# One stage's hand-written TensorE order in a hybrid HGRN2 and pooling layer: mean squares placed apart from the pool projections, first two head-branch products interleaved, kept weights later, banks taken in reverse

## The chip, the cores and the metric

The kernel runs on one core of one Trainium2 chip. The metric is device time in microseconds (us) of one launch, lower is better; a time stands beside others as the median of several runs. Five engines work side by side, each through its own queue of instructions in order, and they meet only through semaphores: TensorE (PE in the profile: matmuls from on-chip memory into PSUM banks), VectorE (DVE), ScalarE (ACT), GpSimd (POOL) and SyncE (SP, which here only issues transfers).

## The reference

One layer of a decoder in float32, 1024 tokens of width 1024 with 16 learned tokens ahead of them:

```python
u = rmsnorm(h, mix_norm_pre[l])
proj = u @ w_in[l]
q, f_logit, i_in, g_out, v_pool, gate_a, gate_b = jnp.split(proj, cuts, axis=-1)
a = hgrn2(q, f_logit, i_in, g_out, lbs[l], hgrn_out_norm[l])     # 4 heads of 128
p = multiscale_pool(v_pool, pool_proj[l], pool_scale[l])         # 4 groups of 128
z = (jax.nn.sigmoid(gate_a) * (a @ w_branch_hgrn[l])
     + jax.nn.sigmoid(gate_b) * (p @ w_branch_pool[l]))
h = h + rmsnorm(z @ w_out[l], mix_norm_post[l])
u = rmsnorm(h, ffn_norm_pre[l])
gt = causal_dwconv(u @ ffn_w_gate[l], ffn_conv_w[l], ffn_conv_b[l])
y = (jax.nn.gelu(gt, approximate=True) * (u @ ffn_w_up[l])) @ ffn_w_down[l]
h = h + rmsnorm(y, ffn_norm_post[l])
```

Inside `hgrn2` a head's output is divided by its root mean square over the 128 channels, `o * lax.rsqrt(jnp.mean(o * o, axis=-1, keepdims=True) + EPS)`, then multiplied by a gain and a sigmoid. `multiscale_pool` takes windowed means of `v_pool` and multiplies each group by a 128x128 matrix. Only the order of this work and the PSUM banks it lands in are touched here.

## The kernel before, in words

Every large product is made of three single-pass matmuls: both operands are split into a rounded high part and a rest (`whi`, `wlo` for weights; `hi`, `lo` for activations), and high x high, high x low and low x high are added in PSUM. The split of a weight block is a cast on ACT and a subtraction on DVE. Channels lie on the 128 partitions, and the 1026 tokens that matter lie along the free dimension in three chunks of 342 columns, so one product of this stage fills three PSUM banks.

The stage in question lies between about 385 and 570 us. It is emitted by one loop that reads the string `ORDER`, token by token. On PE the program order is kept as written; the order on ACT, DVE, SP and POOL is chosen by a scheduler at build time from the same program. The tokens:

- `h0` to `h3` take the next of twelve steps of a head: load, start block (L722), six levels of the recurrence (L693, L699), transpose (L754), state (L771), output (L784, L791, L792), and **mean squares**: six matmuls with a matrix of constants into three banks (L801, L802), then on ACT a logarithm per bank (L803) and one exponential (L804), each behind a table load, then a multiplication on DVE (L805).
- `G` with p, q, r, s: a quarter each of a gate projection (18 matmuls, L207, L208, L211); its sigmoids are L625 on ACT.
- `PP0` to `PP3`: pool projections, nine matmuls each; three copies on ACT (L842) and three subtractions on DVE (L843) read the three banks and free them.
- `BB0` to `BB7` and `BA0` to `BA7`: the products with `w_branch_pool` and `w_branch_hgrn`, 36 matmuls each, here in halves a and b (BB) or whole (BA). DVE multiplies each of the three banks by a gate (L881), and for BA adds the other branch (L1186). `sa0` to `sa3` split a head's finished output for BA (ACT and DVE, L835, L836).
- `w0` to `w5`: weights of the next layer part are prepared early and stored away ("kept"): casts on ACT (L924), sums and subtractions on DVE (L922, L925), stores on SP (L939).

The weights of BB and BA come two products to a block: a load on SP (L162), a cast on ACT (L163), a subtraction on DVE (L164). The buffers `wraw`, `whi` and `wlo` have three places each, shared with the kept weights. PSUM has eight banks in this stage; a new bank is the next in turn. Behind BA stands the mix product with `w_out` (results `pm`, from L187 to L189): its weights are loaded by SP (L1219), cast by ACT (L1226), and subtracted by POOL (L1228); ACT and DVE split `z` for it (L1130, L1131). Rows of `x` and of the learned tokens for the residual are loaded by SP beside them (L1269, L1267).

Of the kernel before, what the change touches and what calls it, by code (L numbers as in the profile page):

```python
# [12 lines left out]
ALU = mybir.AluOpType  # L13
# [40 lines left out]
AHEAD = 3  # L54

ORDER = ("h0 h1 PVp0 PVq0 h0 PVr0 h1 PVs0 h0 PVp1 h1 PVq1 h0 PVr1 h1 PVs1 h0 sp0 PVp2 h1 PVq2 h0 sp1 PVr2 h1 PVs2 "
# [4 lines left out]
POOLED = ()  # L61
VLOAD = 8
TRUNC = False
# [6 lines left out]
def trunk_kernel(ctx: ExitStack, tc: tile.TileContext, x, meta_tokens, mix_norm_pre,  # L70
# [4 lines left out]
    act, dve, pool_e, pe = nc.scalar, nc.vector, nc.gpsimd, nc.tensor  # L75
# [20 lines left out]
    def nm(s):  # L96
        cnt[0] += 1
        return f"{s}_{cnt[0]}"
# [7 lines left out]
    def bank(name="ps"):  # L106
        return stage["ps", "p"].tile([P, 512], F32, tag="ps", name=nm(name))
# [39 lines left out]
    def wsplit(src, n_k, n_c, eng=dve):  # L147
        raw = wst.tile([P, n_k * n_c], F32, tag="wraw", name=nm("wraw"), bufs=NRAW, padded_shape=[P, 1024])
        with tc.issue_after(stage["after"].ins) if "after" in stage else nullcontext():
            stage["load"] = nc.sync.dma_start(raw.rearrange("p (k c) -> p k c", k=n_k), src)  # L150
        hi = wst.tile([P, n_k * n_c], F32R, tag="whi", name=nm("whi"), padded_shape=[P, 1024])
        lo = wst.tile([P, n_k * n_c], F32R, tag="wlo", name=nm("wlo"), padded_shape=[P, 1024])
        act.copy(hi, raw)
        eng.tensor_tensor(lo, raw, rr(hi), ALU.subtract)
        return [(hi.rearrange("p (k c) -> p k c", k=n_k), lo.rearrange("p (k c) -> p k c", k=n_k))]
# [11 lines left out]
    class Loader:  # L167
# [10 lines left out]
        def next(self):  # L178
            self.at += 1
            return self.got[self.at - 1]  # L180

    def wblock(w, k0, n_k, c0, n_c):
        return w[k0 * P : (k0 + n_k) * P, c0 : c0 + n_c].rearrange("(k p) c -> p k c", p=P)

    def mm3(ps, a, b, first, last):
        (ahi, alo), (bhi, blo) = a, b
        pe.matmul(ps, ahi, bhi, start=first, stop=False)  # L187
        pe.matmul(ps, ahi, blo, start=False, stop=False)  # L188
        pe.matmul(ps, alo, bhi, start=False, stop=last)  # L189

    def proj(*a, **k):
        for banks in proj_parts(*a, **k):
            pass
        return banks

    def proj_parts(w, col, n_k, xs, chunks, ws=None, name="pj", by_bank=0, cuts=()):

        if ws is None:
            ws, = wsplit(wblock(w, 0, n_k, col, P), n_k, P)
        whi, wlo = ws  # L200
        banks = [bank(name) for _ in chunks]
        for k in range(n_k - by_bank):
            if k in cuts:
                yield banks
            for (lo, n), ps in zip(chunks, banks):
                xhi, xlo = xs(k, lo, n)
                pe.matmul(ps[:, :n], whi[:, k, :], xhi, start=(k == 0), stop=False)  # L207
                pe.matmul(ps[:, :n], whi[:, k, :], xlo, start=False, stop=False)  # L208
            for (lo, n), ps in zip(chunks, banks):
                xhi, _ = xs(k, lo, n)  # L210
                pe.matmul(ps[:, :n], wlo[:, k, :], xhi, start=False, stop=(k == n_k - 1))  # L211
        for (lo, n), ps in zip(chunks, banks):
            for k in range(n_k - by_bank, n_k):
                mm3(ps[:, :n], (whi[:, k, :], wlo[:, k, :]), xs(k, lo, n), False, k == n_k - 1)
        yield banks
# [609 lines left out]
    def pool_split(g):  # L825
        w = POOL_WINDOWS[g]
        cur, vp = pooled[g]
        if w > T0 + 1:
            dve.tensor_scalar(cur[:, T0 : T0 + 1], cur[:, T0 : T0 + 1], float(w) / (T0 + 1), None, ALU.mult)
        dve.scalar_tensor_tensor(cur[:, T0:L], cur[:, T0:L], 1.0 / w, vp[:, T0:L], ALU.mult, ALU.subtract)  # L830
        pin[g] = split(cur[:, T0:L], "pl")

    def split(src, name, eng=dve):
        hi, lo_ = slot(TQ, F32R, name + "h"), slot(TQ, F32R, name + "l")
        act.copy(hi, src)  # L835
        eng.tensor_tensor(lo_, src, rr(hi), ALU.subtract)  # L836
        return hi, lo_
# [10 lines left out]
    sas, sbs, z = {}, {}, {}  # L848
# [44 lines left out]
    def job(kind, i):  # L893
        if kind == "G":
            return (wblock(WIN, 0, KD, CG + i * P, P), KD, u_q, CH_Q, lambda r: post_g(i, r))
        if kind == "PV":
            return (wblock(WIN, 0, KD, CV + i * P, P), KD, u_all, CH_ALL, lambda r: post_pv(i, r))
        if kind == "PP":
            return (pool_proj[0, i].rearrange("(k c) d -> c k d", k=1), 1,
                    lambda k, lo, n: (pin[i][0][:, lo : lo + n], pin[i][1][:, lo : lo + n]), CH_Q,  # L900
                    lambda r: post_pp(i, r))
        if kind == "BA":
            return (wblock(w_branch_hgrn[0], 0, HEADS, i * P, P), HEADS, a_x, CH_Q, lambda r: post_branch(sas, i, r))
        return (wblock(w_branch_pool[0], 0, HEADS, i * P, P), HEADS, p_x, CH_Q, lambda r: post_branch(sbs, i, r))
# [32 lines left out]
    def pay():  # L937
        while owed:
            nc.sync.dma_start(*owed.pop(0))  # L939

    def keep_first(u):
        raw = wst.tile([P, 1024], F32R, tag="wraw", name=nm("wraw"), bufs=NRAW)
        src = rr(raw).rearrange("p (k c) -> p k c", k=KD)
        nc.sync.dma_start(src, wblock(ffn_w_gate[0], 0, KD, 2 * u * P, P))
        keep(((u, "P1"), src[:, :4]), ((u, "P2"), src[:, 4:]), lo=raw)
# [82 lines left out]
    with tc.manual_schedule(engines={E.Activation, E.DVE, E.PE}):  # L1028
# [59 lines left out]
        for h in range(EARLY_G):  # L1088
            src, n_k, xs, chunks, post = job("G", h)
# [51 lines left out]
    with tc.manual_schedule(engines={E.PE}):  # L1141
        for kind, i in order:
            if kind == "sp":
                pool_split(i)
                continue
            if kind == "w":
                keep_first(i) if i < EARLY else next(keeps[i - EARLY])
                continue
            if kind == "sa":
                ahl[i] = split(heads[i]["o"], "a")  # L1150
                continue
            if kind == "h":
                if i not in gens:
                    gens[i] = head_steps(i)
                next(gens[i], None)
                if not loader.at and "after" in stage:
                    loader.ahead()
                continue
            kind, part = kind.rstrip("abpqrs"), kind[-1]
            src, n_k, xs, chunks, post = job(kind, i)  # L1160
            if part in "qr":
                next(halves_of[kind, i])
                continue
            if part in "bs":
                banks = next(halves_of[kind, i])
                loader.ahead()
                pay()
                after[kind, i] = post(banks)
                continue
            if kind in ("BA", "BB"):  # L1170
                load_gate(sas if kind == "BA" else sbs, kind == "BB", i)
            ws = loader.next()
            if (kind, i) == ("BA", KD - 1):
                z0 = [split_z(0, k) for k in range(ZA)]
            if part in "ap":
                halves_of[kind, i] = proj_parts(None, 0, n_k, xs, chunks, ws=ws, name="p" + kind.lower(),
                                                cuts=(n_k // 2,) if part == "a" else range(n_k // 4, n_k, n_k // 4))
                next(halves_of[kind, i])
                continue
            banks = proj(None, 0, n_k, xs, chunks, ws=ws, name="p" + kind.lower(),  # L1180
                         by_bank=2 if (kind, i) == ("BA", KD - 1) else 0)
            loader.ahead()
            pay()
            after[kind, i] = post(banks)
            if kind == "BA":
                dve.tensor_tensor(sas[i], sas[i], sbs[i], ALU.add)  # L1186
                z[i] = sas[i]
# [384 lines left out]
    with tc.manual_schedule(engines={E.PE, E.Activation, E.DVE, E.Pool}):  # L1572
        for i in (1, "m", 0):
            R[i] = Row(0 if i == "m" else HALO + i * P, HALO if i == "m" else P, pair("pm"))
        for c in range(3):
            for at in range(KD - LAST):
                first_, _, then_ = SEAM[c][at].rpartition("|")
# [130 lines left out]
    with tc.manual_schedule(engines={E.Activation, E.DVE}):  # L1708
        for s_ in range(3):
            banks = [[bank("pd") for _ in range(NT)] for _ in range(2)]  # L1710
# [24 lines left out]
    banks = [bank("pd") for _ in range(NT)]  # L1735
# [74 lines left out]
```

## Time and profile before

| what | value |
|---|---|
| runs | 1316.93, 1314.59, 1315.93 us; median 1315.93 |
| profiled execution | 1315.67 us, span 1314.0 us |
| TensorE busy | 1291.8 us, 98% of the span |
| VectorE, ScalarE, GpSimd busy | 962.9, 524.2, 355.1 us (73%, 40%, 27%) |
| mean granted TensorE clock | 0.997 |

The profiled execution is 0.26 us under the median and 1.67 us longer than its span. In rows of instructions the columns are: start in us, duration, engine, line, operation, result and operands, how many were merged, and in square brackets the idle time of that engine just before and what ended it. In the list of waits they are: engine and line that waited, what released it, us in total, times, longest. In a table by stretches each engine has its busy time and in brackets its instructions, and PEclk is the granted clock.

### The profile page before, as it was taken

What the parts mean: (1) busy time and instruction counts of PE and PEld (TensorE: products, weight loads), DVE (VectorE), ACT (ScalarE), POOL (GpSimd) and SP (SyncE); (2) the same over time, 40 slices, a digit from 0 to 9 for tenths busy, and PEclk for the clock granted to TensorE, in tenths of its full rate; (3) what the DMA queues carried; (4) which work ended last, traced back from release to release, by engine and by line L of the source; (5) the groups of instructions that cost most, each with busy time, mean ns of one, the idle gap of its engine ahead of it and who ended that gap; (6) DMA issues with size and microseconds to landing.
All of it is one profiled execution on the core that took longest, in us unless ns stands there. A gap on an engine that the chain in (4) does not pass through costs nothing.

```text
span 1314.0 us, 21961 instructions
## 1 busy us (share of the span) xinstructions
PE 1291.8 (98%) x8650; PEld 1139.7 (87%) x8650; DVE 962.9 (73%) x1293; ACT 524.2 (40%) x905; POOL 355.1 (27%) x307
## 2 busy tenths in 40 slices
PE   8999999999999999999999999999999999999998
PEld 7799899998998898978898888888888888888887
DVE  6768965454775877775588999888998985455758
ACT  5554433332245546236564222232232323444443
POOL 3015333130000000070045555654755652000000
PEclk9999999999999899999999999999999999999999
DMA  8135642325513557797677777668776799666644
GB/s 275 42 106 164 193 162 98 121 90 163 164 68 135 162 177 249 253 334 260 235 267 236 200 209 184 170 193 193 169 181 154 156 260 298 208 224 225 226 174 160
DMA packets 143801, 247.62 MB, mean 188 GB/s; under 512 B 11000, under 2 KB 75164, under 8 KB 143698
## 3 DMA queue, kind: packets, MB, share of 16 engines
q1 hardware_dynamic: 127026, 213.42, 48.4%
q0 software_dynamic: 12064, 24.38, 10.9%
q10 hardware_dynamic: 4608, 8.41, 1.7%
q8 instruction: 68, 1.11, 0.3%
q14 instruction: 35, 0.29, 0.1%
HBM read 174.11 MB, written 95.09 MB: 205 GB/s over the span
## 4 chain that ended last, share of the span: by engine, by line
PE 58%; DMA 3%; ACT 1%; DVE 1%; POOL 1%; issue 0%; SPq 0%; DVEq 0%; ACTq 0%; POOLq 0%
PE P L308 11%; PE P L307 11%; PE P L310 11%; PE pd L187 5%; PE pd L188 5%; PE pd L189 5%; PE pm L188 2%; PE pm L189 2%; PE pm L187 2%; POOL wlo L1228 1%; DMA kept4l<-wraw 1%; DMA wlos<-wlo 1%; PE pba L207 1%; PE pba L208 1%; PE pt L1280 1%; PE pba L211 1%
## 5 line engine op out<-in xcount | busy, mean ns | idle before, releaser
L308 PE MATMUL P<-v,whi 128*128 128x512 f32 (+2 forms) x408 | 140.7, 353 | 0.0
L307 PE MATMUL P<-v,whi 128*128 128x512 f32 (+2 forms) x408 | 140.7, 352 | 0.0
L310 PE MATMUL P<-v,wlo 128*128 128x512 f32 (+2 forms) x424 | 135.1, 349 | 0.0
L278 POOL TENSOR_TENSOR swa<-wraw,wraw 128x512 f32<-128x512 f32 x32 | 48.2, 1507 | 190.4 <-DMA wraw<-in_ffn_w_gate_dram 71.2
L252 ACT CAST whi<-wraw 128x512 fp32r<-128x512 f32 x90 | 53.1, 618 | 101.7 <-PE P L308 86.9
L1520 DVE TENSOR_TENSOR rot<-wraw,rot 128x1024 fp32r<-128x1024 f32 x31 | 37.9, 1224 | 72.3 <-ACT rot L1519 72.3
L307 PEld LDWEIGHTS P<-v,whi 128*128 128x128 f32 x408 | 76.7, 188 | 10.4
L308 PEld LDWEIGHTS P<-v,whi 128*128 128x128 f32 x408 | 76.6, 188 | 10.2
L310 PEld LDWEIGHTS P<-v,wlo 128*128 128x128 f32 x424 | 74.0, 188 | 10.8
L189 PE MATMUL pd<-rot 128*128 128x512 f32 x274 | 82.5, 388 | 0.0
L188 PE MATMUL pd<-rot 128*128 128x512 f32 x274 | 82.5, 388 | 0.0
L187 PE MATMUL pd<-rot 128*128 128x512 f32 x274 | 81.9, 388 | 0.1
L253 DVE TENSOR_TENSOR wlo<-wraw,whi 128x512 fp32r<-128x512 f32 x86 | 75.2, 896 | 2.7 <-ACT whi L252 2.7
L252 ACT CAST whi<-swa 128x512 fp32r<-128x512 f32 x64 | 38.1, 618 | 90.9 <-PE P L308 80.3
L253 DVE TENSOR_TENSOR wlo<-swb,whi 128x512 fp32r<-128x512 f32 x64 | 67.0, 1054 | 8.8 <-ACT whi L252 8.7
L1519 ACT CAST rot<-wraw 128x1024 fp32r<-128x1024 f32 x31 | 32.7, 1054 | 90.7 <-PE pd L189 89.4
L307 PE MATMUL P<-uhi,whi 128*128 128x258 f32 (+2 forms) x240 | 68.6, 303 | 0.1
L308 PE MATMUL P<-ulo,whi 128*128 128x258 f32 (+2 forms) x240 | 68.4, 303 | 0.0
L252 ACT CAST whi<-swb 128x512 fp32r<-128x512 f32 x64 | 38.1, 618 | 69.1 <-PE P L308 64.6
L307 PE MATMUL P<-t2h,whi 128*128 128x258 f32 (+2 forms) x228 | 65.3, 304 | 0.3 <-DVE sg L864 0.3
L307 PE MATMUL P<-t4h,whi 128*128 128x258 f32 (+2 forms) x228 | 65.5, 304 | 0.0
L308 PE MATMUL P<-t4l,whi 128*128 128x258 f32 (+2 forms) x228 | 65.4, 304 | 0.0
(386 smaller groups left out, 3841.4 us busy)
## 6 DMA issues: line engine op xcount, KB each, us to landing
wraw<-in_w_in_dram SPq DMA_DIRECT2D x36, 512.0 KB, 4.7
yt<-ysum SPq DMA_DIRECT2D x33, 512.0 KB, 5.5
wraw<-in_ffn_w_gate_dram SPq DMA_DIRECT2D x26, 512.0 KB, 6.2
wraw<-in_ffn_w_up_dram SPq DMA_DIRECT2D x22, 512.0 KB, 6.7
wsum<-in_ffn_w_down_dram SPq DMA_DIRECT2D x22, 512.0 KB, 8.3
wraw<-in_w_out_dram SPq DMA_DIRECT2D x18, 512.0 KB, 5.1
ysum<-ys SPq DMA_DIRECT2D x11, 768.0 KB, 5.7
sa<-sscr SPq DMA_DIRECT2D x16, 513.0 KB, 6.4
```

The source lines that it names most:

```text
L187: pe.matmul(ps, ahi, bhi, start=first, stop=False)
L188: pe.matmul(ps, ahi, blo, start=False, stop=False)
L189: pe.matmul(ps, alo, bhi, start=False, stop=last)
L207: pe.matmul(ps[:, :n], whi[:, k, :], xhi, start=(k == 0), stop=False)
L252: act.copy(hi, src)
L253: (pool_e if 4 <= i < 2 * self.early else dve).tensor_tensor(lo, src, rr(hi), ALU.subtract)
L278: pool_e.tensor_tensor(s1, a21, a22, ALU.add)
L307: pe.matmul(d, whi[:, k, :], xh[:, c : c + w], start=(k == 0 and onto is None), stop=False, **go)
L308: pe.matmul(d, whi[:, k, :], xl[:, c : c + w], start=False, stop=False, **go)
L310: pe.matmul(x[:, o : o + w], wlo[:, k, :], xh[:, c : c + w], start=False, stop=(k == 3), **go)
L1519: act.copy(hi, src)
L1520: dve.tensor_tensor(lo, src, rr(hi), ALU.subtract)
```

## The change

Three edits. The string `ORDER` is rewritten from the last quarters of G on. The mean squares of heads 0 and 1 no longer follow a pool projection: quarters of G or a level stand ahead of them, and the projections follow closer on each other, `PP1`, a level, `PP2`, `PP3`. The weights `w0` and `w1` move from between BB1 and BB3 to behind the first halves of BB4 and BB5, and `w2` behind BA2 together with the last `w5`. `BA0` and `BA1` become halves: first halves of both, then second halves, so that four heads are consumed in pairs. The loop, which so far added the other branch only to whole BA products, gets the same addition for halves. Last, the list of three banks of a projection is reversed, so that the first chunk goes into the bank that was taken last.

```diff
 ORDER = ("h0 h1 PVp0 PVq0 h0 PVr0 h1 PVs0 h0 PVp1 h1 PVq1 h0 PVr1 h1 PVs1 h0 sp0 PVp2 h1 PVq2 h0 sp1 PVr2 h1 PVs2 "
-         "h0 PVp3 h1 PVq3 h0 sp2 PVr3 h1 PVs3 h0 Gp2 h1 h2 Gq2 h0 sp3 Gr2 h1 Gs2 h0 h2 h3 Gp3 h1 PP0 h0 Gq3 h2 h3 "
-         "PP1 h1 Gr3 h2 PP2 h3 Gs3 h2 PP3 h3 BBa0 h2 BBb0 h3 BBa1 h2 BBb1 h3 w0 BBa2 h2 BBb2 h3 w1 BBa3 h3 h2 BBb3 "
-         "h3 h2 BBa4 sa0 w4 BBb4 h2 h3 BBa5 sa1 w4 BBb5 h3 h2 BBa6 w4 BBb6 h3 sa2 BBa7 w5 BBb7 w5 sa3 BA0 w5 BA1 w5 "
-         "BA2 w2 BA3 w3 BA4 BA5 BA6 BA7")
+         "h0 PVp3 h1 PVq3 h0 sp2 PVr3 h1 PVs3 h0 Gp2 h1 h0 h2 Gq2 h1 sp3 Gr2 h0 h2 Gs2 h3 h1 Gp3 h0 h2 Gq3 h3 PP0 "
+         "Gr3 h2 h1 Gs3 h3 PP1 h2 PP2 PP3 h3 BBa0 h2 BBb0 h3 BBa1 h2 BBb1 h3 BBa2 h2 BBb2 h3 BBa3 h2 h3 BBb3 h2 h3 "
+         "BBa4 w0 BBb4 h2 h3 BBa5 w1 BBb5 h3 BBa6 h2 sa0 BBb6 sa1 w4 BBa7 h3 w4 BBb7 sa2 BAa0 w4 BAa1 sa3 w5 BAb0 "
+         "w5 BAb1 w5 BA2 w5 w2 BA3 w3 BA4 BA5 BA6 BA7")
...
-        banks = [bank(name) for _ in chunks]
+        banks = [bank(name) for _ in chunks][::-1]
...
                 after[kind, i] = post(banks)
+                if kind == "BA":
+                    dve.tensor_tensor(sas[i], sas[i], sbs[i], ALU.add)
+                    z[i] = sas[i]
                 continue
```

Lines behind the insertion count three higher in the changed kernel (L1186 is L1189, L1219 is L1222, L1226 is L1229, L1228 is L1231, L1267 is L1270). The number of instructions is the same on every engine.

On PE, where head 0's mean squares (`ms`) stand: before, directly behind the pool projection PP0 (`ppp`).

```order
L211 MATMUL ppp_4573<-plh_3869,wlo_4250 128x342
L211 MATMUL ppp_4574<-plh_3869,wlo_4250 128x342
L211 MATMUL ppp_4575<-plh_3869,wlo_4250 128x342
L801 MATMUL ms_4603<-rh_4461,onesr 128x342
L802 MATMUL ms_4603<-rl_4462,onesr 128x342
L801 MATMUL ms_4607<-rh_4461,onesr 128x342
```

In the changed kernel, on PE, the same for head 0: a quarter of G (`pg`) stands ahead.

```order
L211 MATMUL pg_4554<-uhi_88,wlo_4087 128x342
L211 MATMUL pg_4553<-uhi_88,wlo_4087 128x342
L211 MATMUL pg_4552<-uhi_88,wlo_4087 128x342
L801 MATMUL ms_4573<-rh_4433,onesr 128x342
L802 MATMUL ms_4573<-rl_4434,onesr 128x342
L801 MATMUL ms_4577<-rh_4433,onesr 128x342
```

The mean squares moved ahead of the pool projection, and with them the banks that they are given; the descending numbers of `pg` are the reversed banks.

On ACT at the end of the stage, before: the cast of the weight `w2` (`x2`), the cast for BA6 and BA7 (L163), and the splits of `z` (`zc`).

```order
L924 CAST whi_5998<-wraw_5996 128x512 x2
L163 CAST whi_6045<-wraw_6044 128x1024
L1130 CAST zc_6207<-sa_5830 128x256
L1134 CAST zc_6207<-sa_5830 128x2
L1130 CAST zc_6212<-sa_5889 128x256
L1134 CAST zc_6212<-sa_5889 128x2
```

In the changed kernel, on ACT, from the last split of `z` ahead of the same two casts on:

```order
L1130 CAST zc_6222<-sa_6001 128x256
L1134 CAST zc_6222<-sa_6001 128x2
L924 CAST whi_5996<-wraw_5994 128x512 x2
L163 CAST whi_6043<-wraw_6042 128x1024
L924 CAST whi_6061<-wraw_6059 128x512 x2
L1130 CAST zc_6361<-sa_6066 128x256
```

The four splits of `z` have moved ahead of both casts. The cast of `w2` still stands ahead of the one for BA6 and BA7, but the place in `whi` that it takes is now that of the block for BA4 and BA5, so it waits for the last high-part matmul of BA5; before, it waited for that of BA3.

On SP near the end, before: loads of `w_out` (L1219), the stores of `w3` (`kept`), the rows of `x`, and the learned tokens (L1267).

```order
L1219 DMA wraw_6290<-in_w_out_dram 128x1024
L939 DMA kept2h<-whi_6061 128x512
L939 DMA kept4h<-whi_6061 128x512
L939 DMA kept2l<-wraw_6059 128x512
L939 DMA kept4l<-wraw_6059 128x512
L1219 DMA wraw_6294<-in_w_out_dram 128x1024
L1269 DMA row_797_6330<-in_x_dram 128x1024
L1269 DMA row_798_6332<-in_x_dram 128x1024
L1267 DMA row_799_6334<-in_meta_tokens_dram 2x1024
```

In the changed kernel, on SP, the same loads:

```order
L1272 DMA row_798_6332<-in_x_dram 128x1024
L1222 DMA wraw_6290<-in_w_out_dram 128x1024
L939 DMA kept2h<-whi_6061 128x512
L939 DMA kept4h<-whi_6061 128x512
L939 DMA kept2l<-wraw_6059 128x512
L939 DMA kept4l<-wraw_6059 128x512
L1270 DMA row_799_6334<-in_meta_tokens_dram 2x1024
L1222 DMA wraw_6294<-in_w_out_dram 128x1024
```

The second load of `w_out` has moved behind the rows of `x` and behind the learned tokens' load, which in both kernels waits for the high-part matmuls of BA7's first quarter.

## The prediction, as put on record before the result was known

> **What bounds the kernel now.** I read the page first, its busy times.
>
> ```profile
> PE 1291.8 (98%) x8650; PEld 1139.7 (87%) x8650; DVE 962.9 (73%) x1293; ACT 524.2 (40%) x905; POOL 355.1 (27%) x307
> ```
>
> TensorE is busy for 1291.8 of 1314.0 us. No matmul is added or taken away, so the change can only move the 22 us in which TensorE stands still, and the stretches in which its clock is low. Next, the waits of TensorE between 340 and 600 us, the stage of the change:
>
> ```profile
> PE ms L801 <- DVE near L714: 2.9, 1, 2.9
> PE pbb L207 <- ACT rs L803: 2.2, 1, 2.2
> PE sl L693 <- DVE q L682: 1.5, 1, 1.5
> PE ms L801 <- DVE uhi L843: 1.3, 1, 1.3
> PE ms L802 <- DVE rl L836: 0.8, 1, 0.8
> PE pm L188 <- POOL wlo L1228: 0.6, 1, 0.6
> PE ms L801 <- DVE near L724: 0.5, 1, 0.5
> PE sl L699 <- ACT sg L625: 0.2, 1, 0.2
> ```
>
> Four of the eight are mean squares that wait for a bank or an operand, and one (L207 on L803) is a product that waits for the banks of mean squares. The timeline of TensorE shows the largest, and the table by stretches what it does to the clock:
>
> ```profile
> 428.66 0.62 PE L801 MATMUL ms<-rh,onesr 128*128 128x342 f32 x1 [2.94 <-DVE near L714]
> 514.51 0.42 PE L207 MATMUL pbb<-uhi,whi 128*128 128x342 f32 x1 [2.21 <-ACT rs L803]
> ...
> 420.00:428.00 8.00, 5.72 (x155) 5.18 (x154) 5.03 (x6) 7.94 (x12) 0.00 (x0) 0.98 0.15 42
> 428.00:434.00 6.00, 4.86 (x16) 4.49 (x17) 4.69 (x10) 3.98 (x6) 0.00 (x0) 0.50 0.24 67
> 434.00:440.00 6.00, 6.00 (x156) 5.52 (x155) 4.38 (x7) 2.85 (x5) 0.00 (x0) 0.96 0.09 26
> ```
>
> In 428 to 434 the granted clock is 0.50; with the 0.98 and 0.96 beside it, half clock lasts from about 427.7 to 434.5. TensorE worked 4.86 us there and some 0.48 us after, so half clock cost (4.86 + 0.48) / 2 = 2.7 us.
>
> **What the change removes.** Head 0's mean squares follow a quarter of G and head 1's a level, so their banks are free in time: 2.9 + 1.3 + 0.5 us go, and with the order of G the 0.2. Between BBa3 and head 3's sixth level stands head 2's transpose now, and w0 and w1 no longer hold DVE there: 1.5 us go. Head 3's mean squares stand three half products after its output, and their banks are read long before BAa1: 0.8 + 2.2 us go. That is 9.4 us, and the 2.7 us of clock hang on the wait of 2.94: **12.1 us removed**, the ceiling of the gain.
>
> **What it adds, first place: PP1 to BB0.** Now PP1, one level, PP2 and PP3 follow each other, ten banks in a row, and DVE, which frees them (L843), sits in order behind head 1's L805. The rows:
>
> ```profile
> 432.13 1.28 ACT L804 ACT_TABLE_LOAD   x1
> 433.42 1.06 ACT L804 ACTIVATE rs<-rs 128x1026 f32<-128x1026 f32 x1
> 437.60 1.05 ACT L163 CAST whi<-wraw 128x1024 fp32r<-128x1024 f32 x1 [3.12 <-PE ppp L208]
> 438.55 1.41 ACT L842 ACTIVATE uhi<-ppp,par 128x342 fp32r<-128x342 f32 x3
> 443.65 1.15 ACT L625 ACTIVATE sg<-pg 128x342 f32<-128x342 f32 x3
> ...
> 434.51 1.23 DVE L805 TENSOR_TENSOR o<-o,rs 128x1026 f32<-128x1026 f32 x1 [1.82 <-ACT rs L804]
> 443.26 1.21 DVE L164 TENSOR_TENSOR wlo<-wraw,whi 128x1024 fp32r<-128x1024 f32 x1
> 444.16 0.74 PE L699 MATMUL sl<-q,k 128*32 128x16 f32 x64 [0.15 <-ACT sg L625]
> ...
> 444.40 0.69 DVE L676 TENSOR_TENSOR k<-k,f 128x528 f32<-128x528 f32 x1
> 447.57 0.56 DVE L843 SCALAR_TENSOR_TENSOR uhi<-ppp,par,uhi 128x342 fp32r<-128x342 f32 x1
> ```
>
> Count from the end of head 1's mean squares. ACT: last logarithm 0.5, table 1.28, exponential 1.06: 2.8. DVE: L805 to 4.1, then head 3's first level (two operations of 0.69 and some small ones, 2.3) to 6.4. ACT meanwhile needs a small cast, a table load, the three sigmoids of 1.15 and the cast L163 of 1.05, to 6.6, and DVE's L164 waits for that: to 7.8, one L676 to 8.5, the first L843 of PP1 to 9.05. TensorE meanwhile runs a quarter of G, a level, PP1, a level and PP2, 18 + 9 + 9 matmuls at 0.159 us (below) and two levels of 0.7: 7.15. PP3's first pair of matmuls ends at 7.5, its second bank is PP1's first: it waits 1.6. The third bank waits for a level's L714 behind one more L682: 0.6. BBa0's second bank waits behind two L843, the next L164 and one L843: 0.9, its third 0.45. Sum **3.6 us**, in pieces of 1.6 at most. Bounds: none if DVE comes through earlier, and 4.9, what the four waits cost that stood here.
>
> **Second place: BAb0.** Its last quarter needs head 3's low part. In DVE's order L805 of head 3 is followed by three L881, an L836, an L925, the L164 for BA2 and then the L836 that it waits for:
>
> ```profile
> 536.76 1.35 DVE L881 TENSOR_TENSOR sa<-sa,pba 128x342 f32<-128x342 f32 x3 [1.44 <-PE pba L211]
> 542.49 1.35 DVE L881 TENSOR_TENSOR sa<-sa,pba 128x342 f32<-128x342 f32 x3 [0.91 <-PE pba L211]
> 522.29 1.22 DVE L836 TENSOR_TENSOR al<-o,ah 128x1026 fp32r<-128x1026 f32 x1
> ```
>
> The two L881 stand one product apart: 5.73 us for 36 matmuls, 0.159 each. The exponential of head 3 ends 4.5 us after its mean squares; 1.2 + 1.3 + 1.2 + 0.7 + 1.2 + 1.2 more make 11.3. TensorE needs the low part after BBb7, BAa0, BAa1 and nine matmuls, 18 x 3 + 9 at 0.159, and one: 10.2. **1.1 us**; bounds none and 2.2, the wait that stood here.
>
> w0 and w1 moved: their casts, and behind them the cast L163 for BA0 and BA1, stand on ACT ahead of head 2's output copies, and each waits for the stores of the one before to land.
>
> ```profile
> 464.63 1.14 ACT L924 CAST whi<-wraw 128x512 fp32r<-128x512 f32 x2 [4.17 <-DMA kept1h<-whi]
> ```
>
> Two such pairs and L163 make 2 x (1.14 + 4.17) + 1.05 = 11.7 us from the end of BBb3. TensorE asks for the first bank that those copies free after BB4 (5.7 us) and four head steps (two states, a transpose, an output; some 9 us by their distances in the timeline): hidden with 3 us to spare, and past that it costs what the landings take longer.
>
> **Third place: BA6.** Its weights are cast behind w2's cast, and that now waits for BA5. The trace of before shows the same sequence, with w2 waiting for BA3:
>
> ```profile
> 542.34 1.14 ACT L924 CAST whi<-wraw 128x512 fp32r<-128x512 f32 x2 [2.12 <-PE pba L208]
> ...
> 543.76 1.29 DVE L925 TENSOR_TENSOR wraw<-wraw,whi 128x512 fp32r<-128x512 f32 x2
> 544.97 1.22 DVE L1186 TENSOR_TENSOR sa<-sa,sa 128x1026 f32<-128x1026 f32 x1
> 546.33 1.23 DVE L164 TENSOR_TENSOR wlo<-wraw,whi 128x1024 fp32r<-128x1024 f32 x1
> ```
>
> The cast starts 0.2 us after the product's last L208, 0.27 us before the product ends. L924 x2 and L163 (1.05 above; its load is there by now) end 1.9 us behind the product; BA6 starts after 2.0. Its six high-part matmuls run 0.95, then L211 needs L164, which in DVE's order stands behind L881 x3, L925 x2 and the addition: 4.75 behind the product. A second wait of 1.8. **3.8 us**, where before the same block was ready 9 us ahead. Bounds: 2.0 if only the cast counts, and 5.2, all of the sequence.
>
> **Fourth place: the second mix step.** SP now issues the second load of w_out behind the learned tokens' load.
>
> ```profile
> 556.78 0.33 SPq L1219 DMA_DIRECT2D wraw<-in_w_out_dram  x1
> 560.96 0.25 SPq L1267 DMA_DIRECT2D row<-in_meta_tokens_dram  x1
> ...
> 564.96 1.05 ACT L1226 CAST whi<-wraw 128x1024 fp32r<-128x1024 f32 x1 [2.60 <-DMA wraw<-in_w_out_dram]
> 566.10 2.38 POOL L1228 TENSOR_TENSOR wlo<-wraw,whi 128x1024 fp32r<-128x1024 f32 x1 [0.45 <-ACT whi L1226]
> 565.50 0.39 PE L187 MATMUL pm<-whi,zc 128*128 128x512 f32 x1
> 569.16 0.39 PE L187 MATMUL pm<-whi,zc 128*128 128x512 f32 x1
> ...
> kept4h<-whi SPq DMA_DIRECT2D x1, 256.0 KB, 10.0
> wraw<-in_w_out_dram SPq DMA_DIRECT2D x18, 512.0 KB, 5.1
> ```
>
> L1267 was issued 4.54 us before the mix began (565.50). A load issued there that lands after t is cast and subtracted 3.6 us later, and the second step needs it 3.9 us after the mix begins (569.16, plus one matmul): the wait is t - 4.9. With the page's 5.1 it is **0.2 us**; the bounds are none and, with 10.0, 5.1. I take the low end, since the rows of x that stood behind this load are ahead of it now and drained.
>
> **Reversed banks** only change which chunk waits; counted above.
>
> Sum: -12.1 + 3.6 + 1.1 + 3.8 + 0.2 = -3.4, so 1315.67 - 3.4 = 1312.3 in the profiled execution's terms; that stands 0.26 under the median of the runs, so **1312.5 us**.
>
> A rule speaks on the clock. The row: half clock began about 2.0 us into a wait of 2.94 us, and a wait of 2.21 us (514.51) did nothing. The Trainium skill, "TensorE: Matmul & The Clock Gate", in its part on the clock gate, says half rate follows at least one idle window of about 3.4 us, and warns of gaps over about 3 us. The trace is sharper: it fell at less. By the page alone no wait named above lowers the clock, and the result would stay 1312.5. By the row BA6's two waits, 3.8 us within 4.75, may, at the 2.7 us of the stretch above.
>
> **Rivals.**
>
> B, the first two places cost nothing: TensorE's waits there hang on DVE's rank order, and in the trace ACT and DVE have slack between 434 and 440. Then 1312.5 - 3.6 - 1.1 = 1307.8. Against it: the waits follow from the order on DVE, whatever the durations.
>
> C, the clock falls once, at BA6 or in PP3 (2.2 us of wait within 2.6): 2.7 more, 1315.2. For it: 427.7 fell with as little. Against: 514.51.
>
> D, slower: the second load of w_out lands late, as transfers around 550 us did (10.0 above). Waits of 1.2 for the cast and more for POOL sum to 5.1 with hardly a matmul between, so the clock falls as it did for 2.94, 2.7 more: 1312.5 - 0.2 + 7.8 = 1320.1. It decides from a wait of 2.9, t = 7.8, where the total passes 1317.9. Against it: the queue is emptier by 1 MB.
>
> **Chances.** Forecast as summed 0.40, B 0.17, C 0.25, D 0.18. About 0.2%, 2.6 us, is what a measurement of this kernel can tell from no change: faster is under 1313.3, slower over 1318.6. The forecast's own range, 1310 to 1314.5, gives 0.30 faster and 0.10 same; B is faster; C same 0.22, slower 0.03; D slower 0.15, same 0.03. Faster 0.47, same 0.35, slower 0.18. The range takes in B and most of D: 1307.5 to 1319.5.
>
> **What would show it.** In the waits after: no mean square on L714 or L843; L207 `ppp` on L843 with 1 to 2 us; L207 and L211 `pba` on L163 and L164 with about 2 us each near the end of BA; `pm` on POOL or ACT under 1 us. Granted clock 1.00 around 428; at BA6 it tells C. The forecast is wrong if BA6 does not wait, if the first place costs nothing or far more, or if a mix step waits over 2 us.

## The result, and the profile after

| kernel | median us | lowest to highest | ratio to before, 95% interval |
|---|---|---|---|
| before | 1315.56 | 1313.42 to 1316.93 | |
| the change | 1320.29 | 1319.05 to 1322.11 | 1.0037 [1.0026, 1.0049] |

The change is slower by 0.37%, 4.7 us in the medians. It was forecast 3.4 us faster; the time lies outside the range. The profiled execution took 1320.58 us with a span of 1318.9, 4.9 us longer than before, so the profile holds the whole difference.

First the waits of TensorE between 340 and 610 us in the changed kernel: engine and line that waited, what released it, us in total, times, longest.

```profile
PE pba L207 <- ACT whi L163: 8.5, 1, 8.5
PE pm L188 <- POOL wlo L1231: 3.2, 3, 1.7
PE ppp L207 <- DVE uhi L843: 1.2, 1, 1.2
PE pba L208 <- DVE al L836: 0.8, 1, 0.8
PE ppp L207 <- DVE near L714: 0.3, 1, 0.3
PE pba L207 <- DVE sa L881: 0.3, 1, 0.3
```

Of the eight waits that stood in this list before, seven are gone, the mean squares and L207 on L803 among them; the eighth, `pm` on POOL, has grown from 0.6 to 3.2. The list comes to 14.3 us where it was 10.0, and 8.5 of them are one wait: the product BA6 on the cast of its weights. The table by stretches shows the granted clock (the column behind the five engines).

```profile
420.00:435.00 15.00, 14.77 (x327) 13.49 (x314) 12.15 (x21) 12.32 (x21) 0.00 (x0) 1.00 0.65 199
435.00:442.00 7.00, 5.69 (x83) 4.95 (x84) 7.00 (x15) 4.51 (x8) 0.00 (x0) 0.76 0.99 313
546.00:553.00 7.00, 0.00 (x0) 0.00 (x0) 5.56 (x13) 0.44 (x1) 0.00 (x0) 0.59 1.05 395
553.00:558.00 5.00, 4.34 (x16) 4.10 (x17) 3.78 (x5) 1.75 (x3) 0.00 (x0) 0.56 1.04 334
```

The half clock around 428 is gone too, as forecast. But the clock falls at two new places: behind PP3, where 7 us at 0.76 cost at most 1.7, and at BA6, where TensorE stands still for 7 us and then works 4.34 us at about half clock, 1.9 lost. So clock and waits together: 3.6 + 14.3 = 17.9 now, 2.7 + 10.0 = 12.7 before, 5.2 more, where the spans differ by 4.9.

Where the 8.5 us come from is in the chain of waits that ended last (start, us, what):

```profile
517.18 4.85 DMA kept7h<-whi
...
522.38 0.63 ACT whi L924
...
524.15 0.61 DVE wlo L925
524.78 7.62 DMA kept4l<-wlo
...
532.49 1.30 DVE wlo L922 x2
...
537.95 0.63 ACT whi L924
538.59 0.32 SPq L939
...
540.10 7.25 DMA sa<-sscr
...
547.44 1.35 DVE sa L881 x3
```

The last store of w4 (kept7h) has to land before w5's first cast can take its place, 522.38. That piece's last store (kept4l) has to land, 7.62 us, before the first sum of w5's second piece (L922) can write, 532.49. The third piece is cast at 537.95 and its store issued on SP at 538.59; behind it in SP's order stand the loads of BA6's weights (539.00) and of the gates of BA, one of which, issued at 540.10, lands 7.25 later and holds an L881 until 547.44.

The timelines of ACT, TensorE and SP have the end of it:

```profile
544.75 1.14 ACT L924 CAST whi<-wraw 128x512 fp32r<-128x512 f32 x2 [0.75 <-PE pba L208]
552.56 1.05 ACT L163 CAST whi<-wraw 128x1024 fp32r<-128x1024 f32 x1 [6.67 <-DVE sa L881]
553.66 0.65 PE L207 MATMUL pba<-ah,whi 128*128 128x342 f32 x1 [8.48 <-ACT whi L163]
...
542.95 1.45 SPq L939 DMA_DIRECT2D kept8h<-whi  x1
552.56 0.33 SPq L939 DMA_DIRECT2D kept3h<-whi  x1
```

The cast of w2 ends at 545.9, as forecast; the cast for BA6 starts 6.67 us later. The trace names an L881 of DVE as its releaser, but that operation touches none of the cast's operands. In the program the cast waits for its own loads, for a subtraction of w5's third piece (an L925, over by 542.6), and for the store kept8h of that piece, which reads the `whi` place that the cast overwrites. SP issued this store at 542.95. A second instruction waits for the same store: SP's next kept3h, which takes up its semaphore. It went out at 552.56, in the same instant as the cast began. The same two instructions start together in three more kernels of this document: at 554.86 and 554.85 with the tail alone, at 551.75 with w0 and w1 back, at 550.86 without the reversal. In the control below, where SP's order differs, the load of a gain starts with the cast in the other's stead (550.70). So the store took some 9.6 us, and it is what held BA6, as far as a trace can tell that names another operation; runs below test it.

### The profile page after: what moved, and what is told of

Its sections match the earlier page's. It is cut to its first block, busy times and chain, and to the rows that moved or that the text cites. A ratio compares the mean times of both kernels' runs of the same rounds, so it can differ in the third digit from the quotient of the medians.

```text
span 1318.9 us, 21954 instructions
## 1 busy us (share of the span) xinstructions
PE 1292.7 (98%) x8650; PEld 1140.0 (86%) x8650; DVE 956.6 (73%) x1293; ACT 524.6 (40%) x905; POOL 353.3 (27%) x307
## 4 chain that ended last, share of the span: by engine, by line
PE 91%; DMA 3%; DVE 2%; POOL 1%; ACT 1%; issue 1%; SPq 0%; DVEq 0%; POOLq 0%; ACTq 0%
PE P L307 17%; PE P L308 17%; PE P L310 17%; PE pd L187 5%; PE pd L188 5%; PE pd L189 5%; PE pm L188 2%; PE pm L189 2%; PE pm L187 2%; PE ppv L207 1%; PE pbb L207 1%; POOL wlo L1231 1%; PE pv L188 1%; PE ppv L211 1%; PE pv L187 1%; PE ppv L208 1%
## 5 line engine op out<-in xcount | busy, mean ns | idle before, releaser
L1451 DVE SCALAR_TENSOR_TENSOR y<-g,par,y 128x1024 f32<-128x1024 f32 x44 | 65.6, 1491 | 0.8
```

The costliest lines, as they stand in the source:

```text
L1451: dve.scalar_tensor_tensor(a, g[:, j : j + SEQ], cvw[:, j, m : m + 1], a, ALU.mult, ALU.add)
```

## The experiments

In the diffs a line shows a piece of the string `ORDER`. All kernels compute the whole reference. Each ratio is to runs of the kernel before on the same chip (medians 1314.5 to 1315.6).

### Front and tail apart

The change up to PP3 with the old order behind it, and the old order up to PP3 with the change's behind it; both with reversed banks.

```diff
 front_only
-... h3 BBa0 h2 BBb0 h3 BBa1 h2 BBb1 h3 BBa2 h2 BBb2 h3 BBa3 h2 h3 BBb3 h2 h3 BBa4 w0 ...   (the change's)
+... h3 BBa0 h2 BBb0 h3 BBa1 h2 BBb1 h3 w0 BBa2 h2 BBb2 h3 w1 BBa3 h3 h2 BBb3 h3 h2 BBa4 sa0 w4 ...   (before's)
 tail_only
-... Gp2 h1 h0 h2 Gq2 h1 sp3 Gr2 h0 h2 Gs2 h3 h1 Gp3 h0 h2 Gq3 h3 PP0 Gr3 h2 h1 Gs3 h3 PP1 h2 PP2 PP3 h3 ...
+... Gp2 h1 h2 Gq2 h0 sp3 Gr2 h1 Gs2 h0 h2 h3 Gp3 h1 PP0 h0 Gq3 h2 h3 PP1 h1 Gr3 h2 PP2 h3 Gs3 h2 PP3 h3 ...
```

> Only the part of the order up to PP3 is new, and the reversed banks; from BB0 on everything stands as before (w0, w1, w4, w5 early, BA0 and BA1 whole). Store theory (BA6's cast waits for the landing of a kept-weight store of w5, which comes late only because the kept weights were moved behind): no wait at BA6, the mean-square waits of heads 0 and 1 (4.9 us) and their half clock (2.7 us) gone against 1.5 us at PP3 and some 1.5 us of clock there, so 4 to 5 us faster than before, about 1311. Order theory of the prediction: the same here. Rival (the front is what made the end late, since everything arrives earlier at transfers that are not earlier): a wait of several us at BA6 or in the mix steps, 1316 or more.

> The order up to PP3 as before, from BB0 on as in the change, banks reversed. Store theory: the waits on head 0's and 1's mean squares stay (4.9 us and 2.7 us of clock), 4.5 us go (1.5, 0.8, 2.2), and the wait of about 8.5 us at BA6, some 3 us in the mix steps, 1 us at BA0 and BA1 and 1.7 us of clock come: about 1325. Rival (the front is what made the end late): BA6 waits under 4 us, 1316 or less.

Measured: the front alone 1311.24 us, ratio 0.9966 [0.9954, 0.9979]; the tail alone 1323.29 us, 1.0061 [1.0049, 1.0074]. TensorE's largest wait in the tail alone is 7.2 us, BA6 on L163 again. So the front gains what the forecast gave it (4.1 us in the spans; 4.9 + 2.7 - 3.6 = 4.0 by its steps), though not piece by piece: the waits that it adds at PP3 and BB0 are 1.8 us, not 3.6, and the clock falls once more behind the wait of L207 on L803 that the old tail keeps. All of the loss is in the tail.

### The reversed banks

```diff
 no_reverse, from the change
-        banks = [bank(name) for _ in chunks][::-1]
+        banks = [bank(name) for _ in chunks]
 reverse_only, from the kernel before
-        banks = [bank(name) for _ in chunks]
+        banks = [bank(name) for _ in chunks][::-1]
```

> The change without the reversed banks. The prediction's step: within 1.5 us of the change, 1318.5 to 1321.5, with BA6's wait on the cast of 7 to 9 us. Rival (the reversal is what makes the front or the end wait): 1317 or less, or 1323 and more.

> Before with the reversed list of banks and nothing else. The prediction's step: only which chunk waits changes, so the time stays within 1.5 us of before, 1314 to 1316.5, and the mean squares of head 0 and head 1 still wait. Rival (the first chunk in the bank taken last delays or hastens the frees): over 2.6 us either way.

Measured: the change without the reversal 1319.26 us, 1.0032 [1.002, 1.0044]; before with the reversal alone 1315.16 us, 1.0003 [0.9994, 1.0012]. The reversal changes the time of neither kernel beyond the noise. The first kernel's wait at BA6 is 6.3 us, under the 7 to 9 that were expected.

### The kept weights at their old places

The change with w0, w1, w4 and w5 where they stood before or within a half product of it, and w5's last piece ahead of BA2; the front and the halves of BA0 and BA1 stay.

```diff
 kept_early
-BBa2 h2 BBb2 h3 BBa3 h2 h3 BBb3 h2 h3 BBa4 w0 BBb4 h2 h3 BBa5 w1 BBb5 h3 BBa6 h2 sa0 BBb6 sa1 w4
-BBa7 h3 w4 BBb7 sa2 BAa0 w4 BAa1 sa3 w5 BAb0 w5 BAb1 w5 BA2 w5 w2 BA3
+w0 BBa2 h2 BBb2 h3 w1 BBa3 h2 h3 BBb3 h2 h3 BBa4 w4 BBb4 h2 h3 BBa5 w4 BBb5 h3 BBa6 h2 sa0 w4 BBb6 sa1
+BBa7 h3 w5 BBb7 w5 sa2 BAa0 BAa1 sa3 w5 BAb0 w5 BAb1 BA2 w2 BA3
```

> The change with the kept weights w0, w1, w4, w5, w2, w3 back at about the places they had before (w0 behind BBb1, w1 behind BBb2, w4 from BB4 to BB6, w5 from BB7 on, w2 behind BA2); heads, mean squares, pool projections and halves of BA0 and BA1 as in the change. Store theory: no wait over 1 us at BA6, mix steps as before (under 1 us), the 1.5 us at head 3's sixth level may come back: 1308 to 1311. Rival (halves of BA0 and BA1 with their operands arriving in pairs cost the time): 1315 or more, with the wait at BAb0 or BA6.

Measured: **1309.18 us, 0.9954 [0.9941, 0.9968]**, faster than both kernels. No wait is over 1.4 us, and BA6 does not wait at all. What the change lost lies in where the kept weights stand. Which of them it is, two kernels tell: only w0 and w1 moved back, and only w4 and w5 moved back.

```diff
 w01_early (against the change)
-BBb1 h3 BBa2 h2 BBb2 h3 BBa3 ... BBa4 w0 BBb4 h2 h3 BBa5 w1 BBb5
+BBb1 h3 w0 BBa2 h2 BBb2 h3 w1 BBa3 ... BBa4 BBb4 h2 h3 BBa5 BBb5
 w45_early (against kept_early)
-w0 BBa2 h2 BBb2 h3 w1 BBa3 ... BBa4 w4 BBb4 h2 h3 BBa5 w4 BBb5
+BBa2 h2 BBb2 h3 BBa3 ... BBa4 w0 w4 BBb4 h2 h3 BBa5 w1 w4 BBb5
```

> The change with only w0 and w1 back at their places between BB1 and BB3; w4 and w5 stay as late as in the change. Theory one (the loss comes from the last kept weights, w4 and w5, whose stores and loads stand between 524 and 552 us in the change): BA6 still waits for its cast with 6 to 8 us, the time is 1318 to 1321 us. Theory two (w0 and w1 are what pushes everything behind them, so with them in place the transfers drain in time): BA6 waits under 3 us, the time is at most 1315 us.

> The counterpart of the kernel in which only w0 and w1 went back (1321.59 us): here w0 and w1 stay behind BBa4 and BBa5 as in the change, and only w4 and w5 (and with it the order of the last w5 and w2) go back to their places. Theory one (the loss is w4 and w5 alone, and the pieces add): BA6 does not wait for its cast, no mix step waits over 1 us, and the time is 1308 to 1311 us. Theory two (w0 and w1 in front of w4 make its stores late as well, since all share two queues of buffers): BA6 waits 2 us or more, and the time is 1313 us or more.

Measured: with w0 and w1 back 1321.59 us, 1.005 [1.0038, 1.0063]; with w4 and w5 back **1308.88 us, 0.9958 [0.9944, 0.9971]**. Theory one held in both, but for the first's time, which lies 0.6 us over its range. The waits of the first:

```profile
PE pba L207 <- ACT whi L163: 7.8, 1, 7.8
PE pm L188 <- POOL wlo L1231: 4.0, 3, 1.9
```

The late places of w0 and w1 cost nothing that these runs show; those of w4 and w5 cost 1.0037 - 0.9958, 0.8% or about 10 us. Four rows of the kernel with w4 and w5 back, on SP, DVE and ACT, stand against the chain above:

```profile
504.09 0.32 SPq L939 DMA_DIRECT2D kept4l<-wlo  x1
515.04 1.28 DVE L922 TENSOR_TENSOR wlo<-wraw,wraw 128x512 f32<-128x512 f32 x2
538.87 1.05 ACT L163 CAST whi<-wraw 128x1024 fp32r<-128x1024 f32 x1 [2.46 <-DMA wraw<-in_w_branch_hgrn_dram]
539.96 1.23 DVE L164 TENSOR_TENSOR wlo<-wraw,whi 128x1024 fp32r<-128x1024 f32 x1 [0.83 <-ACT whi L163]
```

The first piece of w5 is stored at 504.09 instead of 524.78, the sums of its second begin at 515.04 instead of 532.49, and the cast for BA6 runs at 538.87 instead of 552.56. There it waits for its own load, not for a place. The same bytes move in both; what differs is when. The tables by stretches of 10 us from 500 on (transfer engines' busy share in the column before the last), first with w4 and w5 back, then the change:

```profile
500.00:510.00 10.00, 8.74 (x56) 8.45 (x55) 6.42 (x9) 9.75 (x12) 0.00 (x0) 1.00 0.91 308
510.00:520.00 10.00, 8.93 (x55) 8.41 (x54) 9.37 (x13) 7.12 (x10) 0.00 (x0) 1.00 0.54 186
520.00:530.00 10.00, 10.00 (x64) 10.00 (x65) 8.79 (x15) 1.13 (x2) 0.00 (x0) 1.00 0.59 197
```

```profile
500.00:510.00 10.00, 10.00 (x65) 10.00 (x64) 7.88 (x12) 9.91 (x13) 0.00 (x0) 1.00 0.71 254
510.00:520.00 10.00, 8.88 (x54) 8.30 (x54) 8.08 (x12) 5.25 (x7) 0.00 (x0) 1.00 0.44 143
520.00:530.00 10.00, 10.00 (x65) 10.00 (x64) 8.61 (x14) 2.19 (x3) 0.00 (x0) 1.00 0.98 337
```

At 510 to 520 the transfer engines are about half idle in both. The change has moved less by then (0.71 against 0.91 at 500 to 510) and fills them at 520 to 530 (0.98 against 0.59), just where the store of w5's first piece has to land before the second can begin.

### Is it the store that holds BA6's cast?

In one kernel w2 and w3 move behind BA4 and BA5. In another `whi` has a fourth place, so that the cast no longer waits for that store of w5; for that a general buffer pool gives up one of 26 places, and a control gives up that one alone.

```diff
 w2_late
-w5 BA2 w5 w2 BA3 w3 BA4 BA5 BA6 BA7
+w5 BA2 w5 BA3 BA4 w2 BA5 w3 BA6 BA7
 four_whi and its control slots25
-FM_SLOTS = 26
+FM_SLOTS = 25
 four_whi alone, the same at every use of whi
-        tiles_ = [wst.tile([P, 1024], F32R, tag="whi", name=nm("whi"))]
+        tiles_ = [wst.tile([P, 1024], F32R, tag="whi", bufs=4, name=nm("whi"))]
```

> The change with w2 moved from behind BA2 to behind BA4 and w3 from behind BA3 to behind BA5; nothing else. The cast for BA6 and BA7 then takes the place in whi that BA4 and BA5 leave, and waits for no store. Store theory: the wait of BA6 on that cast falls from 8.5 to about 1 us (1.05 cast plus its start, from the last high-part matmul of BA5), a second one of up to 2 us for the low part; 5 to 7 us faster than the change, about 1314. Rival (its load of w_branch_hgrn, or DVE held by late gate loads, was what came last): the wait stays over 5 us, 1318 to 1321.

> The change with four places for whi in place of three, paid for with one of the 26 work slots; the orders of PE, ACT (but for w2's cast, which moves ahead) and SP up to BA6 stay. The cast for BA6 and BA7 then takes a place that only BA5's last high-part matmul frees, and no store of w5. Store theory: the wait of BA6 on that cast falls from 8.5 to about 1 us. Rival (the load of w_branch_hgrn lands late, or the gate loads hold DVE): it stays above 5 us.

> Control for the kernel with four places: the change with 25 work slots in place of 26 and nothing else. SP's order near the end also changes: the second load of w_out stands ahead of the learned tokens' load again. Store theory: the wait of BA6 on the cast stays at 7 to 9 us and the time within 2 us of the change, about 1320; the mix steps wait less than the change's 3.2 us if the place of that load was what made them wait, as the prediction had it, and the same if what precedes them was.

Measured: w2 later 1315.19 us, 0.9999 [0.9991, 1.0008]; four places 1320.86 us, 1.0046 [1.0031, 1.0062]; the control 1316.94 us, 1.0018 [1.0009, 1.0027]. The cast for BA6 with w2 later, then TensorE's wait for it in the control:

```profile
545.03 1.05 ACT L163 CAST whi<-wraw 128x1024 fp32r<-128x1024 f32 x1 [2.90 <-PE pba L208]
...
PE pba L207 <- ACT whi L163: 6.1, 1, 6.1
```

The rows of the kernel with four places, on ACT, TensorE and DVE:

```profile
547.50 1.04 ACT L163 CAST whi<-wraw 128x1024 fp32r<-128x1024 f32 x1
...
548.60 0.42 PE L207 MATMUL pba<-ah,whi 128*128 128x342 f32 x1 [1.76 <-ACT whi L163]
555.25 1.23 PE L211 MATMUL pba<-ah,wlo 128*128 128x342 f32 x3 [4.96 <-DVE wlo L164]
...
548.08 1.35 DVE L881 TENSOR_TENSOR sa<-sa,pba 128x342 f32<-128x342 f32 x3 [1.72 <-DMA sa<-sscr]
552.72 1.35 DVE L881 TENSOR_TENSOR sa<-sa,pba 128x342 f32<-128x342 f32 x3
553.98 1.22 DVE L164 TENSOR_TENSOR wlo<-wraw,whi 128x1024 fp32r<-128x1024 f32 x1
```

With the place free the cast runs at 547.50, 5.1 us sooner than in the change and 3.2 sooner than in the control (550.70), though its loads were issued 2.5 us later than in the change (541.55 against 539.00). So the loads were not what held it in the change; the store was. With w2 later, where the place is that of BA4 and BA5, the cast starts as soon as BA5's last high-part matmul lets it.

But with four places the time does not fall, and it is 3.9 us above the control's: DVE's L164 for the same block stands in order behind an L881 that waits until 548.08 for a late gate load, behind the splits of `z` and another L881, and BA6's low part now waits 4.96 us for it. Two things behind the same late w5 wait side by side, and taking one away shows the other.

The control missed what was expected of it: it is itself 3.4 us faster than the change (2.5 by the ratios), where within 2 was forecast, and BA6 waits 6.1 us, not 7 to 9. The mix waits 1.9 us instead of 3.2, and the clock does not fall at PP3, which alone is worth 1.7. SP's order differs in it (the second load of `w_out` stands ahead of the learned tokens' again), and which transfer that helps was not taken apart.

With w2 later the time is 5 us shorter: BA6 waits 0.7 us for its cast and 0.4 for the low part, but the mix steps behind it wait 5.0 on L1231 and L881. The lateness moved on to the next that needs a transfer.

### The halves of BA, and a better front

Two variations of the fast kernel kept_early: BA0 and BA1 whole again, and the front with more room between the pool projections.

```diff
 whole_ba
-BBb7 w5 sa2 BAa0 BAa1 sa3 w5 BAb0 w5 BAb1 BA2
+BBb7 w5 sa2 sa3 BA0 w5 BA1 w5 BA2
 spread
-Gq3 h3 PP0 Gr3 h2 h1 Gs3 h3 PP1 h2 PP2 PP3 h3
+Gq3 h1 h3 PP0 Gr3 h2 PP1 Gs3 h3 PP2 h2 PP3 h3
```

> The kernel with the change's front and the kept weights at their old places (1309.18 us), with BA0 and BA1 as whole products again, sa3 ahead of both. If the halves in pairs of heads are worth what the removed waits of mean squares and of L207 on L803 cost (0.8 + 2.2 us), TensorE waits some 2 to 3 us at BA0 for the low part of head 3 and the time is 1311 to 1312.5 us. If the halves are worth nothing, because the place of head 3's mean squares in the order is what counts, it is 1308.5 to 1310 us.

> The kernel with the change's front and the kept weights at their old places (1309.18 us), with head 1's mean squares ahead of PP0 and a quarter of G or a level between each two of PP0 to PP2, so that PP3's banks have more time to be read. If the waits of 1.4 and 0.3 us at PP3 are DVE's lateness behind L805, they go and the time is 1307 to 1308 us. If the mean squares then stand closer to a bank that is not read yet, a wait on L801 or L802 of 1 us or more appears and the time is 1309 us or more.

Measured: whole 1314.92 us, 1.0 [0.9991, 1.0008]; spread 1311.51 us, 0.9972 [0.9963, 0.9981]. TensorE in the first, and the stretch around it:

```profile
518.23 0.65 PE L207 MATMUL pba<-ah,whi 128*128 128x342 f32 x1 [3.15 <-ACT ah L835]
...
516.00:524.00 8.00, 5.16 (x17) 4.80 (x18) 6.40 (x9) 2.19 (x3) 0.00 (x0) 0.57 0.76 237
```

The wait came as expected, 3.15 us, and it also halved the clock: 4.90 of the 5.16 us of work ran at half clock, between 516.9 and 523.7, which lost half of that, some 2.4 more. So the time is above both theories' ranges, and the halves are worth some 6 us (1.0 against 0.9954) where head 3's last step stands as late as here, twice what was expected. The spread front is 2.3 us slower in the medians; it ran on another chip, and the two intervals just meet, so what is sure is that it is not faster. The wait of 1.4 us at PP3 gave way to waits of 0.6 and 0.3, but neither a faster kernel nor a wait on L801 followed: BB0 waits now for DVE to read a bank of the projections, and why DVE is late there was not taken apart.

```profile
441.54 0.42 PE L207 MATMUL pbb<-uhi,whi 128*128 128x342 f32 x1 [1.75 <-DVE uhi L843]
```

## Why the prediction was wrong

**What the change removes, 12.1 us: right.** None of the seven waits that the step named is left, and the clock is at 1.00 from 420 to 435.

**First place, PP1 to BB0, 3.6 us: the term was too high, and a fall of the clock made up for it.** The waits are 1.2 + 0.3 = 1.5 us, on the two operations that were named (L843, L714); BB0 does not wait, so the last two pieces (0.9 and 0.45) were wrong. With the 1.7 us of half clock the place costs 3.2; that this is near the forecast is luck.

**Second place, BAb0, 1.1 us: right,** 0.8, on the low part that was named.

**w0 and w1 hidden: right.** Moving them back gained nothing.

**Third place, BA6, 3.8 us: the step that failed.** Its sequence began right (w2's cast behind BA5, ended at 545.9), but "L924 x2 and L163 (1.05 above; its load is there by now) end 1.9 us behind the product" took the load alone as the condition. The cast also needs a place that w5 holds, and w5's store was in flight until about 552.5. The prediction had this kind of wait in hand, at w0 and w1 (4.17 us on kept1h), and did not ask it of BA6. Measured: 8.5 us of wait and 1.9 of clock in place of 3.8. The second wait, for the low part, does not show; the first covers it, as the run with four places made plain. (By the rows given for it, L164 ends 4.95 us behind the product, not 4.75.) Behind the missed condition is a term that the sum left out: the three pieces of w4 and the four of w5 move too, two to five half products later, and this was costed at nothing, without a word. Their stores, their loads and what stands behind these on SP were never counted; the runs put them at about 10 us. The section on the change lists w0, w1 and w2 as moved; w2 stands behind BA2 in both kernels, and what moved there is w5's last piece.

**Fourth place, the second mix step, 0.2 us: wrong,** 3.2 us on POOL in place of the 0.6 that stood there, 2.6 more. None of it is at the second step. The first waits 1.7: the cast of its weights (565.40) stood behind a store of w3 (kept4h), if the trace names the releaser rightly; two later steps wait 0.65 and 0.91. With w4 and w5 back the mix waits 0.8 us in all. That fits the same lateness, but the second load of `w_out` stands ahead of the learned tokens' there again, so these runs do not part the two. The bound of 5.1 held it, but it was reasoned from one moved load, where the whole queue had moved.

By the prediction's steps with these sizes: -12.1 + 3.2 + 0.8 + 0.3 (an L881 that was not foreseen) + 10.4 + 2.6 = +5.2, as above. Rival D, slower, gave 1320.1, next to the 1320.29 measured, but not for its reason: the mix holds 2.6 of it, BA6 the 10.4. Rival C, a clock that falls once, was too mild: it fell twice. The rule of the Trainium skill weighed there ("TensorE: Matmul & The Clock Gate", Part 1: The HAM clock gate), half rate after at least one idle window of about 3.4 us, is borne out at neither place: at PP3 waits of 1.16 and 0.32 us were enough, and at BA6 the clock fell at 547.20, 2.0 us into the wait of 8.48.

## What to carry to other kernels

Work that runs beside the bottleneck has a latest place as well as a price: before moving it later, follow its buffers and its stores to whoever gets the same place next, and ask what is queued behind its transfers on the issuing engine. Count every token of an order that moves, not the ones that the change is named for. When a buffer is added to free one wait and the time does not fall, look at what is late for the same reason on another engine; the cure is the common cause, here w4 and w5 two to five half products earlier.

## What the runs showed of the hardware that was not expected

The clock does not follow the length of a wait. The same wait, BB's last product on L803, stands in the kernel before (2.21 us) and in the one with the front alone:

```profile
509.17 0.65 PE L207 MATMUL pbb<-uhi,whi 128*128 128x342 f32 x1 [2.23 <-ACT rs L803]
```

Before, the clock stayed at 1.00; with the front alone it fell. At PP3 it is the same: 1.16 and 0.32 us of waits took the change to 0.76 in 435 to 442, and 1.36 and 0.31 left the kernel kept_early at 1.00. So a wait of 1.5 us or more can cost another 1.6 or 1.7 us of half clock or nothing.

What differs is where in a fixed grid the wait falls. In these traces half clock lasts 3.41 us at PP3 and in the kernel with the front alone, 6.83 in the kernel before (427.70 to 434.53) and 10.24 at BA6 (547.20 to 557.44): one, two and three steps of one length. The two falls of the change lie 109.23 us apart, 32 such steps. Cut at this grid, the change at PP3 and at BA6, then kept_early at PP3, at the grid that its only fall, at 1305.50 near its end, gives:

```profile
434.56:437.97 3.41, 1.94 (x20) 1.23 (x24) 3.41 (x8) 2.92 (x6) 0.00 (x0) 1.00 0.99 316
437.97:441.38 3.41, 3.41 (x73) 3.14 (x72) 3.41 (x8) 2.02 (x4) 0.00 (x0) 0.50 1.00 312
543.78:547.20 3.42, 1.40 (x9) 1.12 (x8) 0.24 (x2) 1.36 (x4) 0.00 (x0) 1.00 0.93 320
547.20:550.61 3.41, 0.00 (x0) 0.00 (x0) 3.17 (x8) 0.00 (x0) 0.00 (x0) 0.50 1.03 411
...
435.10:438.51 3.41, 2.19 (x50) 1.62 (x52) 3.41 (x8) 2.93 (x7) 0.00 (x0) 1.00 1.08 355
```

And the wait on L803, in the kernel before and with the front alone:

```profile
509.62:513.03 3.41, 1.84 (x10) 1.41 (x9) 2.46 (x3) 3.36 (x4) 0.00 (x0) 1.00 0.08 28
513.03:516.45 3.42, 1.94 (x12) 1.94 (x13) 2.24 (x5) 3.39 (x6) 0.00 (x0) 1.00 0.82 230
...
505.48:508.89 3.41, 1.45 (x9) 1.16 (x8) 2.45 (x4) 3.37 (x4) 0.00 (x0) 1.00 0.34 101
508.89:512.30 3.41, 3.13 (x11) 3.14 (x12) 2.11 (x4) 3.38 (x6) 0.00 (x0) 0.50 0.90 276
```

Each fall shown follows one step in which TensorE stood partly still. The wait of 2.21 us lies across two steps, with 1.84 and 1.94 us of work, and nothing happens; the one of 2.23 lies almost wholly in one step, with 1.45, and the clock falls at its end. At PP3 the step holds 1.94 us of work in the change and 2.19 in kept_early. Work alone is not the measure, since 1.94 brought a fall in the one place and none in the other. The section of the Trainium skill named above states that the window runs free of the kernel's start; the grid agrees with that, and a step half at work was enough here.

A store of 256 KB took 7.62 us to land in the stretch where the transfer engines' share was 0.98, some 9.6 about the one at 1.05, and 4.85 where it was issued at the end of the one at 0.44. With three places in a buffer the landing of a store three tenants back can so stand on TensorE's path, and the trace may name an operation that merely ended near that time: the one to look for is another instruction with the same condition that started in the same instant.
